# The last tile's attention between the tiles of a gate chunk, and two buffers for a stage's normed rows

## Chip, cores and metric

One core of one Trainium2 chip runs the whole kernel. The metric is device time in microseconds for one execution; lower is better. The kernel before took 2214.87 us, the median of 3 runs (2212.23 to 2216.09).

## The reference, cut to what matters

A decoder trunk of two layers over 1024 rows of 1024 float32 values. Each layer norms its rows, projects them (mixer columns, memory queries, gate), mixes, multiplies by silu(gate) and projects back:

```python
for l in range(DEPTH):                      # DEPTH = 2
    h = rms_norm(x, norm_gain[l])
    cols = h @ w_in_a[j]                    # layer 0; w_in_b in layer 1
    mix = dilated_mixer(...)                # layer 0: three dilated window attentions, merged
                                            # layer 1: gated linear recurrence (hgrn2_mixer)
    mem_out = memory_cross_attention(...)   # 4 heads into 256 memory rows
    y = jnp.concatenate([mix, mem_out], axis=-1) * jax.nn.silu(gate)
    x = x + y @ w_out
```

In layer 0 the mixer runs three groups (window 128 with dilation 1, 512 with 4, 2048 with 16) of 8 heads each, and merges a head's three outputs by their softmax denominators:

```python
alpha = jax.nn.softmax(jnp.stack(lses, axis=0), axis=0)
o = jnp.sum(alpha[..., None] * jnp.stack(outs, axis=0), axis=0)
```

## The kernel before

**Precision and projections.** Weights and rows are split into a rounded part and a remainder (fp32r), and each product is three matmuls (hi times hi, hi times lo, lo times hi). A projection of 512 columns (`project_tiles`) takes four weight pieces and walks the 8 row tiles of 128 rows in pairs; each row tile needs 24 matmuls of 128x512 into one PSUM accumulator "acc", of which there are three (pool pp). When a tile's accumulator is done, the caller's `each(m, ps)` empties it. The matmuls of these projections are on L224 to L226, those of the output projections on L540 to L542.

**Weights.** A plan lists all weight pieces in the order of use. `ahead` loads pieces early on SP's queue (L175) into two "raw" buffers; ScalarE rounds (L147, wh<-raw) and VectorE subtracts (L184, wl).

**Layer 0's attention.** The six passes of `group_order` each project k, v and q of four heads. In each q tile (`each_q`) the head norms, the rotary part and the transposes of this tile are followed by the attention (`attend`) of the tile before, so that the last tile's attention is left over at the end of a pass. In the passes with g = 0, `attend` first fetches the two other groups' outputs of this row tile (`fetch_group`, SP, L733) into the buffers "os" of pool gs, which has two; then come 12 score matmuls (L776 to L778), minimum and exponential (L787 on VectorE, L789 on ScalarE), 8 transposes (L794), copies (L796), 16 value matmuls (L800) into the one accumulator "po", and `merge`: ScalarE scales group 0 (L750, four heads), VectorE adds the other two (L753, four heads of each group), and the merged tile goes to DRAM on ScalarE's queue (L755).

**The second gate chunk.** In the last pass, between the q projection and the leftover attention, `gate_chunk(1, ...)` projects 512 gate columns: sigmoid on ScalarE (L447), product on VectorE (L448), store on ScalarE's queue (L450). Its tiles lie in "qn" of the pool heads (two buffers), which the head norms use too. The leftover attention of tile 7 is called after it.

**The output stage of layer 0** (`out_proj` with `load_a`, `y_a`, `finish_a`) opens the pool outp, in which x1, gainb, ol, gt, yhi, ylo and xn lie; the attention's pools are closed before that. It goes over 24 steps: the memory heads (b0 = 8) for all 8 row tiles, then heads 0 to 3 (b0 = 0), then heads 4 to 7 (b0 = 4). Each step multiplies a loaded output tile by its gate tile (L885), splits it (L147 yhi, L890 or L244 ylo) and runs 24 matmuls. In the last 8 steps `finish_a` norms the finished row tile (`norm_rows`: square with sum on ScalarE, L250; reciprocal root on GpSimd, L156; scaling on VectorE, L254) into the tile "xn", and the transposes of these rows (`put_hT`, L262) follow one step later. The next layer's first projection (`project_v`, "vb") comes behind.

**What sets the order.** The kernel is written for a tile framework: program order is the priority, and a scheduler fixes each engine's queue ahead of the run from a simulated schedule. An instruction of low priority can go ahead of a higher one that isn't ready, each engine then works its queue in order, and a tile gets a buffer when one of its pool is given back.

Of the kernel before, what the change touches and what calls it, by code (L numbers as in the profile page):

```python
# [22 lines left out]
F32 = mybir.dt.float32  # L23
# [7 lines left out]
D = 1024  # L31
# [71 lines left out]
def trunk_kernel(ctx, tc, x, mem, pos, norm_gain, w_in_a, q_gain_a, k_gain_a, qk_gain_t, w_out_a,  # L103
# [10 lines left out]
    gs = ctx.enter_context(tc.tile_pool(name="gs", bufs=2))  # L114
# [36 lines left out]
    def rsqrt(ss, n, div):  # L151

        v = small.tile([128, n], F32, name=f"rv{n}")
        V.tensor_scalar(v[:], ss, 1.0 / div, EPS, op0=OP.mult, op1=OP.add)  # L154
        r = small.tile([128, n], F32, name=f"rr{n}")
        G.tensor_tensor(r[:], v[:], nhalf[:, :n], op=OP.pow)  # L156
        return r
# [43 lines left out]
    def ahead(n):  # L201

        while at_piece[1] < min(at_piece[0] + n, len(plan)):
            ready[at_piece[1]] = piece(plan[at_piece[1]][1])
            at_piece[1] += 1

    def take(key, n):
        ahead(n)
        got = []
        for _ in range(n):  # L210
            assert plan[at_piece[0]][0] == key, (key, plan[at_piece[0]][0])
            got.append(ready.pop(at_piece[0]))
            at_piece[0] += 1
        return got

    def project(pss, lhss, pieces, after=None, order=None):

        n = 2 * len(pieces)
        for i, (wh, wl) in enumerate(pieces):
            for ps, lhs in zip(pss, lhss):  # L220
                for j in range(2):
                    at = 2 * i + j
                    hi, lo = lhs(2 * (order or range(4))[i] + j)
                    T.matmul(ps, hi, wh[:, j, :], start=at == 0, stop=False)  # L224
                    T.matmul(ps, hi, wl[:, j, :], start=False, stop=False)  # L225
                    T.matmul(ps, lo, wh[:, j, :], start=False, stop=at == n - 1)  # L226
            if after:
                after(i)

    def project_tiles(key, lhs, each, order=None):  # L230

        W = take(key, 4)
        for m0 in range(0, NT, 2):
            pss = [pp.tile([128, 512], F32, name="acc") for _ in range(2)]
            project([ps[:] for ps in pss], [lhs(m0), lhs(m0 + 1)], W,
                    (lambda i: ahead(3 + i)) if m0 == NT - 2 else None, order)
            if m0 == 0:
                ahead(2)
            for i, ps in enumerate(pss):
                each(m0 + i, ps[:])  # L240
# [4 lines left out]

    def norm_rows(xt, gain, n, pool, parts=1):

        xn = pool.tile([128, D], F32, name="xn")
        ss = small.tile([128, 1], F32, name="ss1")
        A.activation(xn[:], xt, AF.Square, accum_out=ss[:])  # L250
        r = rsqrt(ss[:], 1, D)
        w = n // parts
        for c in (slice(i * w, (i + 1) * w) for i in range(parts)):
            V.scalar_tensor_tensor(xn[:, c], xt[:, c], r[:], gain[:, c], op0=OP.mult, op1=OP.mult)  # L254
        return xn
# [10 lines left out]
    def head_norm(ps, pool, **kw):  # L266
        sq = pool.tile([128, 4, 128], F32, name="sq", bufs=SQB)
        A.activation(sq[:].rearrange("p h d -> p (h d)"), ps, AF.Square)  # L268
        ss = small.tile([128, 4], F32, name="ss4")
        V.tensor_reduce(ss[:], sq[:], axis=AX.X, op=OP.add)  # L270
        r = rsqrt(ss[:], 4, HD)
        n = pool.tile([128, 4, 128], F32, name="qn", **kw)
        V.tensor_tensor(n[:], ps.rearrange("p (h d) -> p h d", h=4), bc(r[:, :, None], [128, 4, 128]), op=OP.mult)  # L273
        return n

    def heads_T(n):
        t = pT.tile([128, 4, 128], F32, name="pt")
        for h in range(4):
            T.transpose(t[:, h, :], n[:, h, :], ident[:])  # L279
        return t  # L280
# [111 lines left out]
    def rows(scr, g, m):  # L392

        r0, st = tile_rows(g, m)
        return scr[r0:r0 + 127 * st + 1:st, :]
# [17 lines left out]
    def natural_order(spare):  # L413

        for k in range(8):
            for n in ("hi", "lo"):
                src, dst = hts[n][:, k, :], spare[n, k] if k < 2 else hts[n][:, k - 2, :]
                if n == "hi" and k in (1, 2, 4, 5, 7):
                    copy(A, dst.rearrange("p (j r) -> p r j", r=4), src.rearrange("p (r j) -> p r j", r=4))
                else:  # L420
                    copy(V, dst.rearrange("p (j r) -> p j r", r=4), src.rearrange("p (r j) -> p j r", r=4))
        for k in range(2):
            for n in ("hi", "lo"):
                copy(V, hts[n][:, 6 + k, :], spare[n, k])
        hts["at"] = [6, 7, 0, 1, 2, 3, 4, 5]
# [4 lines left out]
    def lhs_group(g, m):  # L430
        if g == 0:
            return lhs_natural(m)
        if g == 1:
            return lhs_natural(m % 4 * 2 + m // 4)
        r0 = 256 * (m % 4) + m // 4
        return lambda k: [hT(n, k)[:, r0:r0 + 255:2] for n in ("hi", "lo")]

    def residue_rows(scr, m):

        return rows(scr, 1, m // 2 + 4 * (m % 2))  # L440

    def gate_chunk(c, by_residue, pool=gs, name="os"):


        def each(m, ps):
            sg = pool.tile([128, 4, 128], F32, name=name)[:].rearrange("p h d -> p (h d)")
            A.activation(sg, ps, AF.Sigmoid)  # L447
            V.tensor_tensor(sg, sg, ps, op=OP.mult)  # L448
            scr = gate_scr[:, c * 512:(c + 1) * 512]
            SQ.dma_start(residue_rows(scr, m) if by_residue else scr[m * 128:(m + 1) * 128], sg)  # L450

        project_tiles(("gate", c), lhs_natural, each)

# [152 lines left out]
    with ExitStack() as sa:  # L606
# [9 lines left out]
        with ExitStack() as s0:  # L616
# [28 lines left out]
            while rest > 0:  # L645
                e = 2.0 ** (math.floor(math.log2(rest)) - 6)
                c = math.floor(rest / e) * e
# [59 lines left out]
        with ExitStack() as s1:  # L707
            vring = s1.enter_context(tc.tile_pool(name="vring", bufs=8))
            at_ = s1.enter_context(tc.tile_pool(name="attn", bufs=2))
            ap_ = s1.enter_context(tc.tile_pool(name="heads", bufs=2))  # L710
# [100 lines left out]
            for Q, g in group_order:  # L811
                if (Q, g) == (0, 0):
                    t = kpool.tile([128, NT, 4, 128], F32R, name="kl")[:].rearrange("p (k m) h t -> p k (m h t)", k=4)
                    natural_order({(n, k): t[:, 2 * i + k, :] for i, n in enumerate(("hi", "lo")) for k in range(2)})
                order = None if g else ROLLED
                kT = kpool.tile([128, NT, 4, 128], F32 if g else F32R, name="kT")
                kl = None if g else kpool.tile([128, NT, 4, 128], F32R, name="kl")
                vv, ql = {}, {}
                lhs = lambda m: lhs_group(g, m)

                def each_k(m, ps):
                    n = head_norm(ps, ap_)
                    rotary(n, g, 1, m)
                    t = heads_T(n)
                    A.activation(kT[:, m], t[:], AF.Copy, scale=gqk[:, g:g + 1])
                    if g == 0:
                        V.scalar_tensor_tensor(kl[:, m], t[:], gqk[:, g:g + 1], kT[:, m].bitcast(F32),
                                               op0=OP.mult, op1=OP.subtract)

                def each_v(m, ps):  # L830
                    vv[m] = vring.tile([128, 512], F32, name="vv")
                    copy(A, vv[m][:], ps)

                def each_q(m, ps):
                    n = head_norm(ps, ap_)
                    rotary(n, g, 0, m)
                    t = heads_T(n)
                    q = at_.tile([128, 4, 128], F32 if g else F32R, name="qT")
                    if g:
                        copy(A, q[:], t[:])  # L840
                    else:
                        ql[m] = at_.tile([128, 4, 128], F32R, name="ql", bufs=1)
                        split_evac(q[:], ql[m][:], t[:])
                    if waiting:
                        attend(Q, g, *waiting.pop(), kT, kl, vv)
                    waiting.append((m, q, ql.get(m), fetch_stats(Q, m) if g == 0 else None))

                project_tiles(("k", Q, g), lhs, each_k, order)
                project_tiles(("v", Q, g), lhs, each_v, order)
                waiting = []  # L850
                project_tiles(("q", Q, g), lhs, each_q, order)
                if (Q, g) == group_order[-1]:
                    wide.close()
                    gate_chunk(1, False, ap_, "qn")
                attend(Q, g, *waiting.pop(), kT, kl, vv)

# [46 lines left out]
    with ExitStack() as sb:  # L905
# [4 lines left out]
        vv = {}  # L910
# [336 lines left out]
```

## Time and profile before

| | us |
|---|---|
| median of 3 runs | 2214.87 |
| the profiled execution | 2214.68 |
| its span, first to last instruction | 2212.5 |
| TensorE busy | 2166.2 |
| VectorE busy | 1068.8 |
| ScalarE busy | 749.4 |
| GpSimd busy | 428.1 |

All times of the trace are counted from the start of the span. PE is TensorE, PEld its weight loads, DVE VectorE, ACT ScalarE, POOL GpSimd, SP the sync engine, which only issues transfers here; SPq and ACTq are transfers issued on these queues. A number in brackets at the end of a timeline row is the idle time of that engine ahead of it, and what ended it. Matmuls are pipelined, so the distance from one start to the next tells more than a matmul's own duration.

### The profile page before, as it was taken

The numbers are of one execution on the slowest core, as the hardware profiler recorded it, in microseconds if no ns is written. First come the engines' busy times: TensorE is split into PE (matmuls) and PEld (weight loads), VectorE is DVE, ScalarE is ACT, GpSimd is POOL, SyncE is SP. The second block draws the span as 40 slices with busy tenths as digits, with TensorE's granted clock in tenths as the row PEclk, the third lists the DMA queues.
The fourth block names the chain that finished last, engine by engine and source line by source line (L and its number), as shares of the span: only waits on it lengthen the run. The fifth ranks groups of instructions, "written<-read, shape, count | busy, mean of one in ns | idle before, by whom it ended". The sixth has DMA issues, their size and how long they took to land. (4 is left out here: it accounts for less than half of the span.)

```text
span 2212.5 us, 29630 instructions
## 1 busy us (share of the span) xinstructions
PE 2166.2 (98%) x11288; PEld 1827.8 (83%) x11288; DVE 1068.8 (48%) x2349; ACT 749.4 (34%) x1502; POOL 428.1 (19%) x664
## 2 busy tenths in 40 slices
PE   8999999999999999999999979999999999999999
PEld 6778888888888888888888857778888888888787
DVE  5646413423423325525824745642657772776443
ACT  4535523423323324323423432232632222232211
POOL 2912212312312312212312100011200000000221
PEclk9999999999999999999999989999999999999999
DMA  6552211211111121112311474420311122112833
GB/s 193 166 143 61 55 39 44 73 48 58 59 40 57 57 66 32 57 53 57 109 51 53 144 222 144 143 94 20 91 53 49 49 63 59 51 48 68 254 117 114
DMA packets 181981, 185.46 MB, mean 84 GB/s; under 512 B 49488, under 2 KB 118352, under 8 KB 181840
## 3 DMA queue, kind: packets, MB, share of 16 engines
q1 hardware_dynamic: 116864, 140.44, 21.3%
q10 hardware_dynamic: 64976, 43.14, 6.1%
q8 instruction: 90, 1.47, 0.3%
q14 instruction: 51, 0.42, 0.1%
HBM read 140.41 MB, written 43.12 MB: 83 GB/s over the span
## 5 line engine op out<-in xcount | busy, mean ns | idle before, releaser
L224 PE MATMUL acc<-wh,hhi 128*128 128x512 f32 x1536 | 605.5, 398 | 3.6 <-ACT wh L147 1.4
L225 PE MATMUL acc<-wl,hhi 128*128 128x512 f32 x1536 | 607.3, 396 | 1.1 <-DVE wl L184 0.9
L226 PE MATMUL acc<-wh,hlo 128*128 128x512 f32 x1536 | 605.6, 397 | 0.0
L156 POOL TENSOR_TENSOR rr<-rv,nhalf 128x4 f32<-128x4 f32 (+1 forms) x152 | 150.8, 992 | 1379.1 <-DVE rv L154 1353.7
L184 DVE TENSOR_TENSOR wl<-raw,wh 128x1024 fp32r<-128x1024 f32 x168 | 210.1, 1252 | 401.9 <-ACT wh L147 400.5
L224 PEld LDWEIGHTS acc<-wh,hhi 128*128 128x128 f32 x1536 | 292.1, 190 | 63.0 <-ACT wh L147 2.1
L225 PEld LDWEIGHTS acc<-wl,hhi 128*128 128x128 f32 x1536 | 292.1, 190 | 60.1 <-DVE wl L184 2.3
L226 PEld LDWEIGHTS acc<-wh,hlo 128*128 128x128 f32 x1536 | 291.5, 190 | 58.7
L147 ACT ACTIVATE wh<-raw 128x1024 fp32r<-128x1024 f32 x168 | 177.7, 1059 | 205.4 <-PE acc L226 63.1
L464 PE MATMUL acc<-hhi,wl 128*128 128x512 f32 x512 | 204.6, 400 | 0.0
L463 PE MATMUL acc<-hlo,wh 128*128 128x512 f32 x512 | 204.6, 400 | 0.0
L462 PE MATMUL acc<-hhi,wh 128*128 128x512 f32 x512 | 203.6, 398 | 0.6 <-DVE ol L475 0.6
L540 PE MATMUL acc<-wh,yhi 128*128 128x512 f32 x384 | 155.0, 407 | 15.7 <-ACT yhi L147 15.5
L541 PE MATMUL acc<-wl,yhi 128*128 128x512 f32 x384 | 152.8, 398 | 0.7 <-DVE wl L184 0.7
L542 PE MATMUL acc<-wh,ylo 128*128 128x512 f32 x384 | 151.2, 399 | 0.2 <-POOL ylo L1198 0.2
L270 DVE TENSOR_REDUCE ss<-sq 128x4 f32<-128x512 f32 x116 | 80.0, 690 | 146.0 <-ACT sq L268 145.7
L268 ACT ACTIVATE sq<-acc 128x512 f32<-128x512 f32 x116 | 69.0, 595 | 182.1 <-PE acc L226 173.3
L789 ACT ACTIVATE pa<-pa,st 128x128 f32<-128x128 f32 (+1 forms) x192 | 84.3, 440 | 113.8 <-DVE st L787 113.8
L273 DVE TENSOR_TENSOR qn<-acc,rr 128x512 f32<-128x512 f32 x116 | 79.8, 691 | 75.3 <-PE pt L279 37.8
L462 PEld LDWEIGHTS acc<-hhi,wh 128*128 128x128 f32 x512 | 96.7, 189 | 19.0 <-DVE ol L475 0.8
L463 PEld LDWEIGHTS acc<-hlo,wh 128*128 128x128 f32 x512 | 96.7, 189 | 18.5
L464 PEld LDWEIGHTS acc<-hhi,wl 128*128 128x128 f32 x512 | 96.7, 189 | 17.9
(224 smaller groups left out, 3054.5 us busy)
## 6 DMA issues: line engine op xcount, KB each, us to landing
raw<-in_w_in_a_dram SPq DMA_DIRECT2D x88, 512.0 KB, 3.9
raw<-in_w_in_b_dram SPq DMA_DIRECT2D x40, 512.0 KB, 3.9
o_scr<-os ACTq DMA_DIRECT2D x48, 256.0 KB, 2.1
raw<-in_w_mem_kv_dram SPq DMA_DIRECT2D x16, 512.0 KB, 4.1
os<-o_scr SPq DMA_DIRECT2D x32, 256.0 KB, 3.4
raw<-in_w_out_a_dram SPq DMA_DIRECT2D x12, 512.0 KB, 4.1
raw<-in_w_out_b_dram SPq DMA_DIRECT2D x12, 512.0 KB, 4.3
gt<-gateb_scr SPq DMA_DIRECT2D x24, 256.0 KB, 5.4
```

Source lines behind the costliest of these rows:

```text
L147: A.activation(dst, src, AF.Copy)
L156: G.tensor_tensor(r[:], v[:], nhalf[:, :n], op=OP.pow)
L184: W_LO.tensor_tensor(lo[:], raw[:], hi[:].bitcast(F32), op=OP.subtract)
L224: T.matmul(ps, hi, wh[:, j, :], start=at == 0, stop=False)
L225: T.matmul(ps, hi, wl[:, j, :], start=False, stop=False)
L226: T.matmul(ps, lo, wh[:, j, :], start=False, stop=at == n - 1)
L462: T.matmul(ps[:], wh[:, k, :], mh, start=k == 0, stop=False)
L463: T.matmul(ps[:], wh[:, k, :], ml, start=False, stop=False)
L464: T.matmul(ps[:], wl[:, k, :], mh, start=False, stop=k == 7)
L540: T.matmul(pss[ch][:], hi[:, k, :], wh[:, j, :], start=k == 0, stop=False)
L541: T.matmul(pss[ch][:], hi[:, k, :], wl[:, j, :], start=False, stop=False)
L542: T.matmul(pss[ch][:], lo[:, k, :], wh[:, j, :], start=False, stop=k == 3)
```

## The change

The gate chunk takes a callable `between`, which it calls once, after its second row tile (m = 1); the last pass hands it the leftover attention of tile 7. The gate's tiles move from "qn" of the pool heads to "os" of the pool gs. In `norm_rows` the tile xn gets two buffers in whatever pool it is in; the pool of the input stage has two by itself, the pool outp had one.

```diff
     def norm_rows(xt, gain, n, pool, parts=1):
-        xn = pool.tile([128, D], F32, name="xn")
+        xn = pool.tile([128, D], F32, name="xn", bufs=2)
...
-    def gate_chunk(c, by_residue, pool=gs, name="os"):
+    def gate_chunk(c, by_residue, between=None):
         def each(m, ps):
-            sg = pool.tile([128, 4, 128], F32, name=name)[:].rearrange("p h d -> p (h d)")
+            sg = gs.tile([128, 4, 128], F32, name="os")[:].rearrange("p h d -> p (h d)")
             A.activation(sg, ps, AF.Sigmoid)
             V.tensor_tensor(sg, sg, ps, op=OP.mult)
             scr = gate_scr[:, c * 512:(c + 1) * 512]
             SQ.dma_start(residue_rows(scr, m) if by_residue else scr[m * 128:(m + 1) * 128], sg)
+            if between and m == 1:
+                between()
...
                 project_tiles(("q", Q, g), lhs, each_q, order)
+                last = lambda: attend(Q, g, *waiting.pop(), kT, kl, vv)
                 if (Q, g) == group_order[-1]:
                     wide.close()
-                    gate_chunk(1, False, ap_, "qn")
-                attend(Q, g, *waiting.pop(), kT, kl, vv)
+                    gate_chunk(1, False, last)
+                else:
+                    last()
```

## Rows read from the trace of the kernel before

**Rows 1.** The page's first part: busy time, share of the span and number of instructions of each engine.
```profile
PE 2166.2 (98%) x11288; PEld 1827.8 (83%) x11288; DVE 1068.8 (48%) x2349; ACT 749.4 (34%) x1502; POOL 428.1 (19%) x664
```
**Rows 2.** What TensorE waited for between 1180 and 1500 us: the tile and line that waited, what ended it, us in total, times, longest.
```profile
PE acc L540 <- ACT yhi L147: 14.6, 3, 13.6
PE pt L794 <- ACT pa L789: 2.6, 1, 2.6
PE pt L262 <- DVE xn L254: 1.9, 1, 1.9
PE acc L224 <- ACT vb L147: 1.2, 1, 1.2
```
**Rows 3.** TensorE's timeline from the gate chunk's end into the output stage: start, us, line, operation, out<-in, shapes, count, idle time ahead.
```profile
1284.68 0.40 PE L226 MATMUL acc<-wh,hlo 128*128 128x512 f32 x1
1284.91 0.28 PE L776 MATMUL s<-kT,qT 128*128 128x256 f32 x1
1285.03 0.28 PE L777 MATMUL s<-kl,qT 128*128 128x256 f32 x1
...
1289.11 1.91 PE L794 MATMUL pt<-ident,pa 128*128 128x128 f32 x8 [2.60 <-ACT pa L789]
...
1306.53 0.79 PE L540 MATMUL acc<-wh,yhi 128*128 128x512 f32 x1 [13.57 <-ACT yhi L147]
...
1307.55 0.63 PE L540 MATMUL acc<-wh,yhi 128*128 128x512 f32 x1
1307.97 0.63 PE L541 MATMUL acc<-wl,yhi 128*128 128x512 f32 x1
```
**Rows 4.** What the transfers on SP's queue waited for between 1200 and 1310 us: us in total, times, longest.
```profile
SPq L733 <- DVE os L753: 36.9, 11, 11.4
...
SPq L143 <- DMA o_scr<-os: 8.3, 1, 8.3
```
**Rows 5.** ScalarE's timeline between the last attention and the output stage.
```profile
1295.62 0.33 ACTq L755 DMA_DIRECT2D o_scr<-os  x1
1305.39 1.08 ACT L147 ACTIVATE yhi<-ol 128x512 fp32r<-128x512 f32 x1 [11.26 <-DMA gt<-gatem_scr]
```
**Rows 6.** Transfers issued between 1290 and 1310 us: count, KB each, median us from issue to landing.
```profile
o_scr<-os ACTq DMA_DIRECT2D x1, 256.0 KB, 2.0
```
**Rows 7.** Stretches of the span: us, then busy time and count of PE, PEld, DVE, ACT and POOL, the granted clock of TensorE as a share of full speed, the DMA share and GB/s.
```profile
1306.50:1312.20 5.70, 5.67 (x14) 4.48 (x15) 3.33 (x4) 2.23 (x2) 0.00 (x0) 0.51 1.09 347
1312.20:1330.00 17.80, 17.80 (x78) 14.31 (x77) 12.19 (x16) 3.52 (x3) 0.00 (x0) 1.00 0.96 305
...
1482.40:1486.30 3.90, 3.90 (x10) 3.12 (x11) 0.15 (x1) 2.20 (x5) 0.89 (x1) 0.52 0.89 279
```
**Rows 8.** TensorE's timeline at the end of the output stage.
```profile
1474.72 1.04 PE L262 MATMUL pt<-ident,xn 128*128 128x128 f32 x8
...
1479.29 1.90 PE L262 MATMUL pt<-ident,xn 128*128 128x128 f32 x8 [1.93 <-DVE xn L254]
1482.36 0.80 PE L224 MATMUL acc<-wh,hhi 128*128 128x512 f32 x1 [1.18 <-ACT vb L147]
```
**Rows 9.** TensorE's timeline within the gate chunk: tile 6's value matmuls and the next gate matmul.
```profile
1263.62 1.95 PE L800 MATMUL po<-vv,pts 128*128 128x128 f32 x16
1265.32 0.48 PE L224 MATMUL acc<-wh,hhi 128*128 128x512 f32 x1
```
**Rows 10.** ScalarE's timeline within the gate chunk.
```profile
1250.91 0.60 ACT L447 ACTIVATE qn<-acc 128x512 f32<-128x512 f32 x1 [2.81 <-DMA gate_scr<-qn]
...
1259.95 1.28 ACT L447 ACT_TABLE_LOAD   x1 [0.94 <-PE acc L226]
1261.24 1.09 ACT L447 ACTIVATE qn<-acc 128x512 f32<-128x512 f32 x2
...
1265.60 1.15 ACT L750 ACTIVATE os<-po,mw 128x128 f32<-128x128 f32 x4 [3.27 <-PE po L800]
```
**Rows 11.** VectorE's timeline within the gate chunk.
```profile
1259.92 0.68 DVE L796 COPY pts<-pt 128x512 f32<-128x512 f32 x1
...
1261.87 0.69 DVE L448 TENSOR_TENSOR qn<-qn,acc 128x512 f32<-128x512 f32 x1 [0.49 <-ACT qn L447]
...
1266.00 2.19 DVE L753 SCALAR_TENSOR_TENSOR os<-os,mw 128x128 f32<-128x128 f32 x8 [2.58 <-ACT os L750]
```
**Rows 12.** TensorE's groups of instructions between 1253.7 and 1285 us: line, out<-in, shapes, count, busy us, mean ns, idle us before them.
```profile
L224 PE MATMUL acc<-wh,hhi 128*128 128x512 f32 x40 | 15.9, 397 | 0.0
L225 PE MATMUL acc<-wl,hhi 128*128 128x512 f32 x40 | 15.7, 392 | 0.0
L226 PE MATMUL acc<-wh,hlo 128*128 128x512 f32 x41 | 15.7, 394 | 0.0
```
**Rows 13.** Transfers issued between 1255 and 1275 us: count, KB each, median us from issue to landing.
```profile
os<-o_scr SPq DMA_DIRECT2D x4, 256.0 KB, 3.1
gate_scr<-qn ACTq DMA_DIRECT2D x3, 256.0 KB, 2.3
```
**Rows 14.** ScalarE's timeline at the end of the output stage: the square of the last tile.
```profile
1476.33 1.07 ACT L250 ACTIVATE xn<-x 128x1024 f32<-128x1024 f32 x1
```
**Rows 15.** VectorE's timeline at the end of the output stage: the last tile's last add, and tile 6's normed rows.
```profile
1465.03 0.68 DVE L547 TENSOR_TENSOR x<-x,acc 128x512 f32<-128x512 f32 x1
...
1469.58 1.28 DVE L254 SCALAR_TENSOR_TENSOR xn<-x,rr,gainb 128x1024 f32<-128x1024 f32 x1
```

## The prediction, made before the change was run

> **What bounds the kernel now.** I read the page first, then the waits of TensorE around the two places that the diff names, then the timelines there. TensorE is busy 97.9% of the span [rows 1], so time can be won only where it stands still or runs at half clock, and the reader should look for nothing else. Between 1180 and 1500 us it waits 14.6 us for the first operands of the output projection (L540), 2.6 us for the last attention's probabilities (L794), 1.9 us for the last normed rows (L262) and 1.2 us for a free accumulator of the next layer (L224) [rows 2]. The first two belong to one seam, the end of the second gate chunk; the last two to another, the end of the output stage.
>
> **Seam one, as it is.** The gate's last matmul starts at 1284.68. Only then come the last tile's 12 score matmuls (1284.91), 2.60 us of idleness while the softmax runs, 8 transposes and 16 value matmuls, then 13.57 us of idleness; the output projection starts at 1306.53 [rows 3]. The long gap is a chain: the last merge's store, issued at 1295.62 and 2.0 us in landing, then the first load of the new stage, held 8.3 us by exactly that store, and the first yhi at 1305.39 [rows 4 to 6]. I read this as memory: the output stage's tiles lie where the attention's lay, and its loads wait until the last attention tile is given back. When TensorE resumes, its granted clock is 0.51 for 5.7 us, the 1.2 GHz level, and 1.00 after that [rows 7]; neighbouring matmuls start 0.42 us apart instead of 0.23 [rows 3].
>
> **What moving the last attention removes.** Its work on TensorE stays. At full clock it is 12 scores at 0.12 from start to start (1.4 us [rows 3]), 8 transposes (1.0 [rows 8]) and 16 value matmuls (1.7 to the next start [rows 9]): 4.1 us. So without any wait the gate would end at 1284.9 + 4.1 = 1289.0. Before, the projection starts at 1306.5 and loses 13 x 0.2 = 2.6 us in the half-clock stretch (5.7 us at 0.43 a matmul) [rows 3, 7]. The ceiling of the move is 1306.5 + 2.6 - 1289.0 = **20.1 us**. The loads of the output stage need 1305.39 - 1295.62 = 9.8 us from the last merge's store to the first yhi [rows 5]; if that store goes out some 20 us before the gate's end, they are all hidden behind gate matmuls. Their cover is the rest of the gate chunk (27 us below); with none they would cost the 13.57 us again. The last tile's two fetches on SP's queue, its store on ScalarE's and its merge are the same instructions as before, moved ahead of gate tiles 2 to 7 and, on SP, of the last weight loads; GpSimd has none of it.
>
> **What it adds: a queue for two buffers.** The diff also moves the gate tiles from the buffer "qn" of the heads pool to "os" of gs, and those two buffers are what every attention of this group fetches its two other group outputs into. In program order the users now are: the two fetches of tile 6, gate tiles 0 and 1, the two fetches of tile 7, gate tiles 2 and 3, and on. That ring is already tight: SP's fetch waits up to 11.4 us for a merge (L753) to finish reading [rows 4]. Before, gate tile 1 left its accumulator at 1250.91, tile 0 still earlier [rows 10]. Now both must wait until tile 6's merge, which runs from 1266.00 to 1268.19 on VectorE [rows 11], has read its first fetch (half of it, 1267.1). There are three accumulators, so the gate can put tiles 0, 1 and 2 into them and then stops. After 1253.7 the trace still has 121 of its 192 matmuls [rows 12], so the three tiles are full at about that time, and TensorE has only small attention work until tile 0 is out.
>
> When is that? Tile 5's value matmuls stood behind gate matmuls on TensorE, and tile 6's behind them; its ScalarE part at 1265.60 waited 3.27 us for them [rows 10]. Tile 6's value matmuls start at 1263.62, 3.0 us behind the copy that feeds them (1259.92 + 0.68) [rows 9, 11]; its transposes queued too, by an estimate 1.2. With the gate matmuls gone these 4.2 us go, and the first buffer is free at 1262.9. Then a table load 1.28, a sigmoid 0.60 and a product 0.69 [rows 10, 11]: the accumulator is free at **1265.5**. From there 120 matmuls at 0.23 (27.6), the value matmuls of tile 7 (1.7), and a half-clock stretch that I size between the two that the trace shows, 1.7 and 2.6 [rows 3, 7, 8]: 2.1. The gate ends at 1296.9, 7.9 us later than the ceiling supposes. The bounds of this loss are 0 (the scheduler lets a gate tile take a buffer ahead of a fetch; tile 1 before took the buffer that came free first) and 12.1 (tile 6's merge no earlier than before: 1267.1 + 2.6 + 31.4 = 1301.1). I take 7.9, since rows for each part of it exist. The second lap (store 2.3, fetch 3.1, merge 2.2 us [rows 11, 13]) ends near 1275, while tiles 3 and 4 keep TensorE busy for 11 us from 1265.5, so it should cost nothing.
>
> On the table load a page speaks against the change. The row shows 1.28 us, and the sigmoid starts 0.01 us behind it [rows 10]. The Trainium skill, ScalarE: Activation LUTs, section "What ACT_TABLE_LOAD costs", puts a drain of about 1.38 us on top, 2.66 in all; by that the sum would be 1.4 us later, and the trace doesn't agree. The Trainium skill, Perfetto Trace Analysis, section "Optimization Strategy", says that repeated gaps on the engine that should be full can mean too few buffers for the next tile; the fetch wait above is such a place, and the page's rule would turn the move into the wait that I have priced.
>
> **The second pair of normed rows.** At seam two the square of the last tile (ScalarE, 1476.33) writes into the one buffer xn, which the transposes of tile 6 read until 1475.8; its input was there at 1465.7, the end of the add [rows 8, 14, 15]. So the last tile is 10 us late, and TensorE shows it: it runs dry at 1477.36, stands 1.93, transposes at half clock in 1.90 instead of 0.9, stands 1.18 for an accumulator that ScalarE empties only behind these transposes, and runs nine matmuls at 0.43 [rows 7, 8]. From 1477.36 to 1486.3 that is 8.9 us for 3.0 us of work: **5.9 us** at most. With two buffers the square follows the add, and the normed rows are there by 1472.3 (after tile 6's on VectorE [rows 15]). If the transposes keep their place in TensorE's queue, behind the matmuls that end at 1477.36, the evacuation of the accumulator still comes after them, and only 1.93 + 1.0 = 2.9 us go; if they come earlier, all 5.9. I take the middle, **4.4**. Below nothing I don't go: no instruction is added, and 4 KB of memory are the price. The other users of norm_rows have two buffers already.
>
> **Sum.** The profiled execution took 2214.68 us (2212.5 of span and 2.2 around it), 0.2 under the median of 2214.87. 2214.7 - 20.1 + 7.9 - 4.4 = **2198.1**.
>
> **Rivals.**
> - The ring as priced (forecast, 0.60): 2192.7 (loss 4, rows 5.9) to 2203.8 (loss 12.1, rows 2.9).
> - The ring costs nothing (0.20): gate tiles slip in between fetches, or tile 6's merge comes well before. Then 2214.7 - 20.1 - 4.4 = 2190.2. For it: buffers go to whoever is ready, as tile 1 showed [rows 10]. Against: a fetch is always ready, and it stands earlier in the program.
> - The ring costs two stops (0.10): tile 6's merge stays where it was, and store and fetch of the second lap take twice their time, so that tile 2 holds its accumulator past tile 4: some 3 us beyond 12.1, and 2.9 for the rows, 2207.
> - Slower (0.06): the first stop drops the clock, and the broken flow keeps it at half to the end of the gate. 120 matmuls cost 0.2 more each, 23.6 instead of 2.1: 2219.6. It turns the change into a loss once some 94 matmuls run at half clock. For it: a gap of 1.93 us was enough to lose the level [rows 7, 8]. Against: in both places 13 matmuls or fewer brought it back.
> - The change doesn't do what it says (0.04): the output stage's loads still start only when the gate is done, because something of the attention's memory is held that long. Then the loads' 8 us lie bare behind 1296.9 and its last store, the first yhi comes near 1309, and only the rows are won: about 2213.
>
> **How the numbers follow.** Predicted is the likeliest, 2198.1. The range must leave out at most 0.2: the slower case, the unchanged one and the worst of the two stops fall off above, the best of the free ring below, which gives 2189 to 2206.5. A measurement of this kernel can tell about 0.2% (4.4 us) from no change. Faster than 2210.4 are the first three cases but for a sliver: 0.88; within: 0.06; slower: 0.06.
>
> **What will show it.** Right: no wait at L540 after the gate, first yhi ready before the gate ends, and SP's first load of gainb some 20 us before it; L447 of tile 0 near 1263 and a hole on TensorE between 1254 and 1266 with a clock of about 0.5 around it; the last square of L250 within 2 us of its add, and the L262 wait gone. Wrong: no hole there (the free ring), a second hole near 1280, a half clock through the whole gate, or loads that still start with the last gate store.

## The result, and the profile after

The changed kernel took 2192.14 us (median of 4 runs, 2191.34 to 2194.61), the kernel before 2213.61 us beside it (2212.23 to 2216.09). The ratio is 0.9904, with a 95% interval of 0.9891 to 0.9916: 21 us faster, or 19 to 24. The forecast was 2198.1. The profiled execution took 2192.18 us, with a span of 2190.3.

The page's first part. Against [rows 1] TensorE's busy time fell by 6.8 us, and its idle time from 46.3 us (2212.5 - 2166.2) to 30.9:
```profile
PE 2159.4 (99%) x11288; PEld 1821.6 (83%) x11288; DVE 1069.4 (49%) x2349; ACT 748.2 (34%) x1500; POOL 427.7 (20%) x664
```
TensorE's waits between 1180 and 1500 us, the view of [rows 2]:
```profile
PE acc L224 <- DVE os L448: 1.4, 1, 1.4
PE po L802 <- ACT os L752: 1.2, 1, 1.2
PE acc L224 <- ACT vb L147: 1.2, 1, 1.2
PE pt L796 <- ACT pa L791: 0.3, 1, 0.3
```
The three long waits of before (14.6, 2.6 and 1.9) are gone. In their place stand 1.4, 1.2 and 0.3 in the gate chunk. The 1.2 for vb stayed.

TensorE's timeline, from the last attention's work within the gate chunk to the seam, which answers to [rows 3, 9]:
```profile
1257.05 0.44 PE L796 MATMUL pt<-ident,pa 128*128 128x128 f32 x2 [0.35 <-ACT pa L791]
...
1260.57 2.05 PE L802 MATMUL po<-vv,pts 128*128 128x128 f32 x16 [1.23 <-ACT os L752]
1264.05 0.50 PE L224 MATMUL acc<-wh,hhi 128*128 128x512 f32 x1 [1.43 <-DVE os L448]
...
1291.47 0.39 PE L226 MATMUL acc<-wh,hlo 128*128 128x512 f32 x1
1291.70 0.39 PE L542 MATMUL acc<-wh,yhi 128*128 128x512 f32 x1
```
The gate's last matmul and the projection's first are 0.23 us apart: the seam is closed. The price stands ahead of it, a hole in three pieces. The value matmuls of tile 6 (two rows of eight, near 1255 and 1257) and of tile 7 (the row of 16) lie in it. In the windows of that hole (columns: us, PE busy, count, granted clock, DMA share, GB/s) TensorE is busy 8.9 of 12 us, and the clock never leaves its level of 2.4 GHz:
```profile
1254.00:1262.00 8.00, 6.32 (x46) 1.00 0.35 101
1262.00:1266.00 4.00, 2.58 (x14) 1.00 0.35 131
1266.00:1291.00 25.00, 25.00 (x110) 1.00 0.87 266
```
ScalarE at the same place, which answers to [rows 5, 10]. Gate tile 0's sigmoid waits for VectorE to have read a fetch of tile 6 (L755). The sigmoid at 1270.36 waits 4.85 us for a merge in the same way, in the ring's second lap, but TensorE has no wait there. The first yhi is made 9 us before the gate ends:
```profile
1260.54 1.28 ACT L447 ACT_TABLE_LOAD   x1
1262.56 0.60 ACT L447 ACTIVATE os<-acc 128x512 f32<-128x512 f32 x1 [0.74 <-DVE os L755]
...
1270.36 0.60 ACT L447 ACTIVATE os<-acc 128x512 f32<-128x512 f32 x1 [4.85 <-DVE os L755]
...
1282.37 1.15 ACT L147 ACTIVATE yhi<-ol 128x512 fp32r<-128x512 f32 x1 [6.38 <-DVE ol L889]
```
SP's queue: the output stage's first load goes out 17.7 us before the projection starts.
```profile
1273.99 0.33 SPq L143 DMA_DIRECT2D gainb<-in_norm_gain_dram  x1
```
At the end of the output stage ScalarE squares the last tile 0.04 us behind its add (VectorE, 1447.67 + 0.68), where before it came 10 us late [rows 14, 15]. It copies vb only behind the last hhi:
```profile
1448.39 1.06 ACT L250 ACTIVATE xn<-x 128x1024 f32<-128x1024 f32 x1 [0.71 <-DVE x L549]
...
1460.64 0.60 ACT L147 ACTIVATE hhi<-pt 128x512 fp32r<-128x512 f32 x1 [3.77 <-PE pt L262]
1461.13 1.57 ACT L147 ACTIVATE vb<-acc 128x512 f32<-128x512 f32 x3
```
TensorE there, the view of [rows 8]: the transposes wait for nothing, and only the accumulator's 1.18 us are left. Of the last tile's eight transposes four go early, between matmuls of the next layer (1455.64), and four behind the last of these that are ready (1460.00).
```profile
1453.80 0.60 PE L262 MATMUL pt<-ident,xn 128*128 128x128 f32 x4
...
1455.64 0.60 PE L262 MATMUL pt<-ident,xn 128*128 128x128 f32 x4
...
1460.00 0.60 PE L262 MATMUL pt<-ident,xn 128*128 128x128 f32 x4
1461.78 0.51 PE L224 MATMUL acc<-wh,hhi 128*128 128x512 f32 x1 [1.18 <-ACT vb L147]
```

**Where the time went.** A caution on single profiles comes first. After is 2.0 us ahead already at a pair of transposes (L279) near 1100 us (1098.36 against 1100.37), although every engine's queue holds the same instructions in the same order up to the gate chunk. The eight profiles of this study that have the move pass that point between 1097.88 and 1101.81, and 1.9 of the 2 us are there by the 1001st matmul (216.90 against 218.75). So they belong to the execution and not to the change. Stated against that point, the 50th and the 384th matmul of the projection start 14.6 and 15.5 us earlier than before (1303.97 against 1320.60, 1386.48 against 1404.03, less 2.0 each). Most of the rise between the two is a wait of before that is gone: 0.66 us for a weight half (L541, at 1364.37). At the end the spans differ by 22.2 us, or 20.2 without the 2.0, so 4.6 of it lie behind the 384th matmul.

### The profile page after: what moved, and what is told of

It reads as the page before. It is cut to its first block, busy times and chain, and to the rows that moved or that the text cites. A ratio compares the mean times of both kernels' runs of the same rounds, so it can differ in the third digit from the quotient of the medians.

```text
span 2190.3 us, 29619 instructions
## 1 busy us (share of the span) xinstructions
PE 2159.4 (99%) x11288; PEld 1821.6 (83%) x11288; DVE 1069.4 (49%) x2349; ACT 748.2 (34%) x1500; POOL 427.7 (20%) x664
## 5 line engine op out<-in xcount | busy, mean ns | idle before, releaser
L184 DVE TENSOR_TENSOR wl<-raw,wh 128x1024 fp32r<-128x1024 f32 x168 | 209.4, 1247 | 388.0 <-ACT wh L147 387.0
L466 PEld LDWEIGHTS acc<-hhi,wl 128*128 128x128 f32 x512 | 96.3, 188 | 17.7
```

The lines of the kernel that those rows point to most:

```text
L184: W_LO.tensor_tensor(lo[:], raw[:], hi[:].bitcast(F32), op=OP.subtract)
L466: T.matmul(ps[:], wl[:, k, :], mh, start=False, stop=k == 7)
```

## The experiments

Theory: seam one was won because the gate tiles left the heads' memory, so that the output stage's loads start with the end of the attention. The ring of two buffers takes part of it back. Seam two is a matter of the second pair of rows alone, and what is left of it is again memory.

**One part alone: the move.** The changed kernel with one buffer for the rows:
```
-        xn = pool.tile([128, D], F32, name="xn", bufs=2)
+        xn = pool.tile([128, D], F32, name="xn")
```


> The change without its second part: the attention moved between the gate tiles and the gate tiles in the shared buffers, but one buffer xn. Theory (the two seams add up): the whole change gave 21.5 us, of which the trace puts 4.7 at the second seam, so this one gives 16.8 and takes about 2196.8 us, with the wait of L262 for the normed rows back at 1.9 us. Rival (the rows are worth only the 2.9 us of their idle time, the clock comes back by itself): 2195.0. Rival (without the first gap the second seam shifts and closes by itself): 2192.

Measured: 2197.37 us (2196.84 to 2198.12), before 2213.95 beside it, ratio 0.9927 (0.9914 to 0.9939): 16.6 us. At the end of the stage the wait of before is back, 1.94 us, and the 1.17 behind it:
```profile
1462.45 1.62 PE L262 MATMUL pt<-ident,xn 128*128 128x128 f32 x8 [1.94 <-DVE xn L254]
1465.25 0.79 PE L224 MATMUL acc<-wh,hhi 128*128 128x512 f32 x1 [1.17 <-ACT vb L147]
```

**The other part alone: the rows.** The kernel before with
```
-        xn = pool.tile([128, D], F32, name="xn")
+        xn = pool.tile([128, D], F32, name="xn", bufs=2)
```


> The kernel before with two buffers xn and nothing else. Theory: idle time of 1.93 us and half-clock transposes (1.0) go, and the half-clock stretch behind them (1.8) too; the 1.18 us wait for the accumulator stays, since ScalarE empties it behind the last tile's transposes: 4.7 us, about 2208.9. Rival (only 2.9 go): 2210.7. Rival (all 5.9 go): 2207.7.

Measured: 2209.93 us (11 runs, 2206.97 to 2211.78), ratio 0.998 (0.9971 to 0.9989): 4.0 us, between the theory's 4.7 and the rival's 2.9, and the time alone can't decide between them. Seam one is as it was:
```profile
1289.20 2.17 PE L794 MATMUL pt<-ident,pa 128*128 128x128 f32 x8 [2.64 <-ACT pa L789]
1307.66 0.80 PE L540 MATMUL acc<-wh,yhi 128*128 128x512 f32 x1 [13.44 <-DMA x<-in_x_dram]
```
At seam two the trace has the theory's picture: the last transposes wait for nothing, the granted clock stays at 1.00, and the 1.18 us for the accumulator are left. Four of the last tile's transposes go early, four stay behind the matmuls:
```profile
1473.71 0.60 PE L262 MATMUL pt<-ident,xn 128*128 128x128 f32 x4
```
The two parts add up: 16.6 + 4.0 = 20.6, against 21.5 for both.

**The move without the change of memory.** The changed kernel, its gate tiles in the buffer "qn" of the heads again:
```
-    def gate_chunk(c, by_residue, between=None):
+    def gate_chunk(c, by_residue, between=None, pool=gs, name="os"):
...
-            sg = gs.tile([128, 4, 128], F32, name="os")[:].rearrange("p h d -> p (h d)")
+            sg = pool.tile([128, 4, 128], F32, name=name)[:].rearrange("p h d -> p (h d)")
...
-                    gate_chunk(1, False, last)
+                    gate_chunk(1, False, last, ap_, "qn")
```


> The whole change, but the gate tiles lie in qn of the pool heads as before, so that the attention's pools are in use until the last gate tile is stored. Theory (the output stage's loads wait for the memory of these pools, whoever uses it last): gainb is loaded only behind the last gate store, some 4 us after the gate's last matmul, TensorE stands 12 us again and falls to half clock; of the first seam only about 5 us are won, 4.7 at the second, 2204. No stop for the shared buffers within the gate. Rival (the attention's own chain at the end was the price, memory isn't): 2188 to 2192.

Measured: 2210.57 us (10 runs, 2205.04 to 2215.59), ratio 0.9989 (0.9979 to 0.9999). That is 3.4 us under the kernel before, and the rows alone bring 4.0: the move's 16.6 us are gone, although the last attention is out of the way. In the trace 0.3 us of them are left at the projection's 50th matmul (1318.78 against 1320.60, less the 1.6 by which this profile is ahead near 1100). ScalarE sends its last merge's store at 1277.77 and the last two gate tiles' at 1291.97:
```profile
1277.77 0.33 ACTq L757 DMA_DIRECT2D o_scr<-os  x1
...
1291.97 0.81 ACTq L450 DMA_DIRECT2D gate_scr<-qn  x2
```
SP's first load of the stage comes only behind the latter, 18.8 us after the merge's store:
```profile
1296.60 0.34 SPq L143 DMA_DIRECT2D gainb<-in_norm_gain_dram  x1
```
and TensorE stands again:
```profile
1305.64 0.80 PE L542 MATMUL acc<-wh,yhi 128*128 128x512 f32 x1 [15.19 <-ACT yhi L147]
```
The gain row's load and the gate tile's store share no data, and yet the load's last 1.8 us of waiting end with that store, which leaves memory as what they share. The rest of the 18.8 us it stands behind three weight loads on SP's queue, which goes in order; the first of them waited 16.8 us for VectorE (L184) and went out at 1288.23. In the changed kernel these loads come behind the gain row's. That the scheduler turned the order because memory came free late is argued, not shown. The forecast of 2204 was 6.6 us too low: TensorE stands 15.2 us and not 12, and next to nothing of the first seam is won, not 5 us. The order alone is worth next to nothing; the buffer is what makes the order count.

**No ring.** One gate buffer of its own, in a pool that is opened ahead of the attention's pools (two work tiles of the heads go down to one buffer each, to make room):
```
-            sg = gs.tile([128, 4, 128], F32, name="os")[:].rearrange("p h d -> p (h d)")
+            sg = pool.tile([128, 4, 128], F32, name="os")[:].rearrange("p h d -> p (h d)")
...
+    own = ExitStack()
+    gg = own.enter_context(tc.tile_pool(name="gg", bufs=1))
...
-                t1 = ap_.tile([128, 4, ROT], F32, name="t1")
-                t2 = ap_.tile([128, 4, ROT], F32, name="t2")
+                t1 = ap_.tile([128, 4, ROT], F32, name="t1", bufs=1)
+                t2 = ap_.tile([128, 4, ROT], F32, name="t2", bufs=1)
...
-                    gate_chunk(1, False, last)
+                    gate_chunk(1, False, last, gg)
```


> The whole change, but the gate tiles get one buffer of their own, in a pool that lives on through the output stage (paid for by one instead of two buffers for two rotary products, which only GpSimd touches, in order). Theory (the 3.1 us for which TensorE stands between 1254 and 1266 are the queue of fetches and gate tiles for two buffers): the gate tiles leave their accumulators early, the hole goes, about 2189 us. Rival (one buffer paces the gate at 4 us of product and store for each tile, and more table loads come in between the exponentials): 2192 or more, with TensorE waiting for L448 elsewhere.

Measured: 2196.18 us (2193.35 to 2197.02), ratio 0.9919 (0.9905 to 0.9932): no gain on the changed kernel, whose median is 4.0 us lower. The forecast of 2189 failed. Yet the hole is gone, and the projection starts 3.7 us earlier (1287.99). It then stops, for weights and accumulators, and loses the clock:
```profile
1287.99 0.39 PE L542 MATMUL acc<-wh,yhi 128*128 128x512 f32 x1
...
1290.57 0.49 PE L542 MATMUL acc<-wh,yhi 128*128 128x512 f32 x1 [1.01 <-ACT wh L147]
1292.45 0.50 PE L543 MATMUL acc<-wl,yhi 128*128 128x512 f32 x1 [1.39 <-DVE wl L184]
...
1294.21 0.60 PE L542 MATMUL acc<-wh,yhi 128*128 128x512 f32 x1 [0.34 <-DVE os L448]
1294.61 0.63 PE L543 MATMUL acc<-wl,yhi 128*128 128x512 f32 x1
...
1301.01 0.50 PE L542 MATMUL acc<-wh,yhi 128*128 128x512 f32 x1 [0.78 <-DVE x L549]
```
In the windows the clock falls to a mean of 0.57, most of the window at the level of 1.2 GHz, with the DMA engines full all the time:
```profile
1290.00:1294.00 4.00, 1.93 (x6) 1.00 1.11 345
1294.00:1298.00 4.00, 3.79 (x10) 0.57 1.07 357
```
The sum closes: 1.01 + 1.39 + 0.34 + 0.78 and nine matmuls at 0.2 more are 5.3 us, and the 50th matmul is 1.6 us later than in the changed kernel (1305.56 against 1303.97), which is 5.3 less the 3.7. At the 384th it is 3.2 us later (1389.68 against 1386.48), behind two more waits of 0.5 us each. Expected had been a gain that the ring held back; shown is that the output stage's start was the next limit, 4 us behind. The edit isn't quite clean: with one buffer for the rotary products the queues differ from the changed kernel's from some 440 us on, but near 1100 us both profiles stand at the same time (1098.42 and 1098.36).

**The ring made longer.** The attention ahead of the whole chunk:
```
-                    gate_chunk(1, False, last)
+                    last()
+                    gate_chunk(1, False)
```


> The changed kernel with one shift: the last tile's attention is issued ahead of the whole gate chunk, and not behind its second tile. The two buffers are then used in the order: fetches of tile 6, fetches of tile 7, gate tile 0, gate tile 1. Ring theory: gate tile 0 must wait until the merge of tile 7 has read its first fetch. In the changed kernel that merge read its two fetches at 1269.2 and 1270.6, where the merge of tile 6 let gate tile 0 go at 1262.6; so TensorE stands some 6.5 us longer ahead of the fourth gate tile, the gate ends 6.5 us later, and the time is 2198.6, or 2200.6 if the longer gap drops the clock for a stretch as gaps of 1.9 us and more did in the kernel before. Rival (a buffer goes to whoever is ready, and gate tile 0 slips in ahead of the fetch): 2192, no change against the changed kernel.

Measured: 2199.8 us (2198.59 to 2202.25), ratio 0.9947 (0.9933 to 0.996), before 2212.03 beside it: 7.7 us over the changed kernel's median, and 6.7 in the profiles (spans 2196.5 and 2190.3, this one 0.5 ahead near 1100). Tile 0's sigmoid waits for the merge of tile 7 and starts at 1267.75 instead of 1262.56, and TensorE has one undivided gap:
```profile
1269.12 0.79 PE L224 MATMUL acc<-wh,hhi 128*128 128x512 f32 x1 [7.01 <-DVE os L448]
1269.71 0.63 PE L225 MATMUL acc<-wl,hhi 128*128 128x512 f32 x1
```
After it the clock is at its lower level (columns as in [rows 7]):
```profile
1270.00:1272.00 2.00, 2.00 (x6) 1.52 (x6) 0.25 (x2) 0.60 (x1) 0.00 (x0) 0.50 0.91 286
```
Eleven matmuls take 4.78 us (1269.12 to 1273.90) where 0.235 each would be 2.6: 2.2 us. The fourth gate tile restarts some 5.5 us later than in the changed kernel (1269.12 against 1264.05, and the 0.5), where 6.5 were forecast; with the 2.2 the projection starts 7.7 later (1298.91 against 1291.70). The ring theory forecast 2200.6 with the clock lost.

**What is left of seam two.** The changed kernel, its rows in a pool of their own:
```
+        xp = s2.enter_context(tc.tile_pool(name="xnp", bufs=2, side="right"))
...
-            xn = norm_rows(x1[:, m, :], gainb[:], D, op, 2 if m == NT - 1 else 1)
+            xn = norm_rows(x1[:, m, :], gainb[:], D, xp, 2 if m == NT - 1 else 1)
```


> The changed kernel, with the two normed rows of the first layer's output stage in a pool of their own instead of the pool of the stage. In the changed kernel TensorE still waits 1.18 us, behind the transposes of the last normed rows, for an accumulator that ScalarE copies to vb only then. Memory theory: those copies go into memory that the stage's pool gives back when its last user, these transposes, is done; with the rows elsewhere two of the copies come earlier, the 1.18 us go, and the time is 1.2 us under the changed kernel: 2190.9. Rival (ScalarE is late there because it is behind with the evacuations of the transposes, whatever the memory): the wait stays, 2192.1.

Measured: 2191.95 us (2191.13 to 2192.45), ratio 0.9908 (0.9894 to 0.9921). ScalarE now copies two vb ahead of the last hhi:
```profile
1455.55 1.09 ACT L147 ACTIVATE vb<-acc 128x512 f32<-128x512 f32 x2 [3.31 <-DMA x_scr<-x]
```
What they wait for there is the store of a finished row tile, with which they share no data: again memory of the stage's pool. TensorE's wait is gone:
```profile
1461.27 0.60 PE L262 MATMUL pt<-ident,xn 128*128 128x128 f32 x4
1461.62 0.48 PE L224 MATMUL acc<-wh,hhi 128*128 128x512 f32 x1
```
This profile is 1.1 us behind that of the changed kernel at the point near 1100 us (1099.45) and has the same span, so the 1.2 us are there in the trace; the medians can't tell them apart from nothing.

**The stage's start, by bytes.** The kernel with a gate buffer of its own, with the gain row's load behind the first three tiles':
```
-        row_bcast(gainb[:], norm_gain[1], D)
...
-        out_proj("out_a", load_a, load_x, y_a, x1, finish_a, op, lambda: None)
+        out_proj("out_a", load_a, load_x, y_a, x1, finish_a, op,
+                 lambda: row_bcast(gainb[:], norm_gain[1], D))
```


> The kernel with one gate buffer of its own, with one shift: the load of the gain row (512 KB, the first load of the output stage) is issued behind the first three tiles' loads and not ahead of them. With the own buffer the gate ended 3.7 us earlier than in the changed kernel (first matmul of the output projection 1287.99 against 1291.70), but by the 50th matmul all of it was lost and more (1305.56 against 1303.97): TensorE waited 1.0 and 1.4 us for weight halves, 0.3 and 0.8 us more, and ran nine matmuls at half clock, while the 16 DMA engines were busy all the time at 320 to 390 GB/s. Traffic theory: the start of the stage is now paced by its own loads; 512 KB at that rate are 1.3 to 1.6 us, so the first products come that much earlier, these waits shrink by about 1.5 us, and with the clock kept by up to 3: 2193 to 2194.7 against 2196.2. Rival (the stage is paced by when its memory comes free, or by ScalarE's order of work, not by bytes): the same time as with the own buffer, 2196.2.

Measured: 2194.6 us (2190.63 to 2197.67), ratio 0.9919 (0.9907 to 0.9931). The median lies in the theory's range, but the kernel before, too, took 1.9 us less beside it (2212.03 against 2213.95); the ratio is the same as without the shift, so the times don't decide. The profile is 3.4 us behind near 1100 us (1101.81 against 1098.42). Against that point the first yhi is 2.7 us earlier (1286.13 against 1285.43), as the traffic theory wants, the clock stays at 1.00, and the 50th matmul is 1.4 us earlier (1307.56), as is the end of the span (2195.7 against 2193.7, less 3.4). But the waits don't shrink: 1.33, 0.34, 0.78, 0.47 and 0.52 are 3.4 us, against 3.5. ScalarE is now idle 7.6 us for the third piece of weights. So the theory has the earlier yhi and not the shorter waits; what is won in the trace is about the price of the half clock. Whether the stage's start is held by the sum of its bytes was argued from the full DMA engines and not shown.

**The same on the changed kernel**: the edit above and that of the own pool for the rows, both on the changed kernel.

> The changed kernel with the normed rows in a pool of their own and the load of the gain row behind the first three tiles' loads. Here TensorE waits only 0.25 us at the start of the output projection, since the gate ends later than the first loads. Theory: the later gain row brings nothing on this base, at most that 0.25: the time of the kernel with the own pool alone, 2190.9 if that one is as forecast. Rival (the loads still cost something that no wait of TensorE shows, such as the stall of ScalarE for raw weights of 6.4 us that follows): 1 us or more under it.

Measured: 2191.18 us (2189.61 to 2192.36), ratio 0.9904 (0.9891 to 0.9918). Theory and measurement agree within the interval: nothing that can be measured. The profile, too, is no more than 0.4 us under that of the own pool alone (spans 2190.2 and 2190.3, near 1100 us 1099.71 and 1099.45). No kernel of the study beats the changed one by more than its measurement can tell.

## Why the prediction came out as it did

The time lies 6.0 us below the forecast and inside its range; a gain of 16.6 us was forecast, and 21.5 are measured. By the number alone the rival of the free ring (2190.2) is nearer. The trace decides against it: the gate's fourth tile waits for the product of tile 0, and that for tile 6's merge, at the place that was named; taking the ring away starts the projection 3.7 us earlier, and making its lap longer costs 7.7. The mechanism was right, and two terms of the ring's price were too large.

- **Ceiling of the move, 20.1: held.** In the projection's first 50 matmuls TensorE waits only 0.25 us, for a weight half, and no clock is lost there.
- **Restart of the gate at 1265.5: right by two errors.** In before's time (2.0 later) it is 1266.1. Tile 6's buffer was free at 1264.5 and not at 1262.9: ahead of the reading that let the sigmoid go, VectorE's queue has one that waited 0.84 us for the second fetch. Against that the table load, 1.28 in the sum, lay in the wait for the buffer (1260.54 to 1261.82, the sigmoid at 1262.56) and cost nothing. With no wait for a buffer, the load of the own-buffer kernel at 1239.43 begins 0.01 us behind the instruction ahead of it and is followed by its sigmoid at 1240.73, 0.02 us behind its end. The Trainium skill, ScalarE: Activation LUTs, section "What ACT_TABLE_LOAD costs", adds a drain of some 1.38 us to every switch of table set; the trace again doesn't agree, with 1.31 us from the end of the instruction ahead of the load to the start of the sigmoid.
- **120 matmuls, 27.6: right.** 1264.05 to 1291.70 are 27.65.
- **Tile 7's value matmuls, 1.7: wrong place.** I put them behind the restart. They ran within the hole, while tile 0 still waited for its buffer, and cost nothing.
- **Half clock, 2.1: didn't occur.** I carried the price of whole gaps [rows 7, 8] over to a hole that the attention's own work breaks into 0.35, 1.23 and 1.43 us. With the same place made one gap of 7.01 us the clock fell and 2.2 us were lost, as priced; the error was in taking the hole for one gap. That the pieces kept the clock because they are pieces isn't shown: the kernel with its own gate buffer lost it behind three short waits.
- So the gate ended at 1293.7 in before's time and not at 1296.9 (+0.6 - 1.7 - 2.1 = -3.2), and the ring cost 4.7 and not 7.9. Of 20.1 this leaves 15.4, and the 50th matmul shows 14.6: the projection's first 49 steps took 12.27 us, where 0.233 each would be 11.4.
- **Second lap at no cost: right.** The waits of 4.85 us on ScalarE never reach TensorE.
- **The rows, 4.4 between 2.9 and 5.9: right in size.** Alone they brought 4.0 us in time; between the 384th matmul and the end the profiles differ by 4.6 us more, of which some 0.5 are shorter waits for the stage's own operands. Neither end of the bound came about: half of the last tile's transposes came early and the half clock went, but the accumulator's 1.18 us stayed. It hangs on memory, as the own pool showed, and not on the transposes' place in the queue, as the prediction had it.
- **Loads that start only with the last gate store** (the rival at 2213) is what the gate tiles in the heads' buffer show: 2210.57.

## What to carry to other kernels

When work is moved to close a gap between stages, ask first whose memory the next stage's loads wait for: the same move was worth 16.6 us with the tiles in a buffer that outlives the stage and nothing that could be measured with them in the old one. Price a ring by who must read before whom, then check what lies behind it: taking the ring away bought 3.7 us at the seam and lost 5.3 at the next stage's first weights. Don't carry the price of a lost clock from one gap over to another: here a hole in three pieces kept the clock, and three short waits at the next stage lost it. Look whether a table load or another engine's small work fits into the wait that you are pricing.

## What the runs showed of the hardware

At one place in the queue, 0.35, 1.23 and 1.43 us of idleness with small matmuls between them, 3.0 of some 9 us, left the granted clock at 1.00, and a single gap of 7.01 us was followed by 0.50. In the kernel with its own gate buffer three short waits (1.01, 1.39 and 0.34 us) within 5 us were followed by 0.57, and a fourth of 0.78 left it at 1.00; with the gain row later, waits of 1.33 and 0.34 at the same place left it at 1.00. Nor does a gap's length settle it. In the kernel before, the 2.60 us ahead of L794 were followed by 1.00 (the mean from 1290.1 to 1293.4); in the kernel with the rows alone, at the same place of the same queue, 2.64 us were followed by 0.50. A wait of 2.04 us in the kernel with the gate tiles in the heads' buffer (at 1268.47) left it at 1.00, while 1.94 at seam two with the move alone was followed by half-clock matmuls, as the 1.93 of the kernel before were [rows 7, 8]. So two profiles can pay differently for the same short gap; why, the runs don't show.

The two kernels with a gate buffer of their own, which differ only in the output stage, were 3.4 us apart by 1100 us (1098.42 and 1101.81). So a difference of 2 us between two profiles must be placed in the span before it is explained.
